# Neighbourhood attention in a hybrid encoder block: a fused bias sum and row maximum, one broadcast normalisation, attention steps in mid-projection, merge additions on VectorE

## The chip, the cores and the metric

The kernel runs on one core of a Trainium2 chip. The metric is the device time of one execution in microseconds (us). A core has five engines that run side by side, each through its own instruction list in order: TensorE (PE, matmuls, with PEld for its weight loads), VectorE (DVE), ScalarE (ACT), GpSimd (POOL) and SyncE (SP, which here issues most DMAs). They wait for one another on semaphores.

## The reference

One layer of an encoder block on 512 tokens of width 1024, in float32. Cut to what matters here:

```python
h = rms_norm(x, mix_norm_g)
proj = h @ w_in            # mLSTM q,k,v,o,gates | attention q,k,v | memory q | merge gates
y_ml = mlstm_branch(...)                         # branch 0 of the kernel
y_xa = memory_cross_attention(xa_q, mem_k, mem_v)   # branch 1
y_na = neighbourhood_attention(na_q, na_k, na_v, na_rpb)   # branch 2
merged = g_ml * (y_ml @ w_br_ml) + g_na * (y_na @ w_br_na) + g_xa * (y_xa @ w_br_xa)
x = x + merged @ w_out
x = x + conv_glu_ffn(rms_norm(x, ffn_norm_g), ...)
return rms_norm(x, final_norm_g)
```

In the neighbourhood attention the tokens form a grid of 8 rows by 64 columns, and there are 8 heads of 64 channels. A token sees all 8 rows and a window of 16 columns; a learned bias, indexed by the relative position, is added to the scores before the softmax:

```python
s = einsum('bhrcd,bhrkjd->bhrckj', q, k_band) * 64 ** -0.5 + bias
s = where(col_ok, s, -inf)
p = softmax(s over all keys of the token)
o = einsum('bhrckj,bhrkjd->bhrcd', p, v_band)
```

The gates `g_*` are sigmoids of 1024 projected channels each.

## The kernel before, in words

Activations lie transposed: 128 channels on the partitions, 512 tokens along the free axis. Float32 accuracy is got from the faster fp32r matmul by splitting both operands into a high and a low part (`wh`, `wl` for weights, `XH`, `XL` for the input); `mm3` (L181) then issues three matmuls, L182, L183 and L184. A projection (`proj`, L328) of one 128-channel block is 8 input tiles by 3 matmuls, 24 matmuls of 128x512, into a PSUM tile `mm`. The weights come as a list of blocks; `weights` (L170) keeps three raw loads (`wr`) and one split ahead. A split is an ACT copy (L164) and a DVE subtraction (L165) for each half block.

The branches are written as generators (`ml_all`, `xa_all`, `na_all`) that yield at the end of each of their steps. `step(n)` (L786) adds n to a quota and runs one generator step for each whole unit. So the generators' work is sprinkled between projections. The instruction lists that result are reordered a little by the scheduler that builds the program, so that some matmuls of a projection come to stand between parts of a step.

The merge loop (L857 to L892) runs over three branches `br`, and for each over four feature pairs `fp`. A pair consists of two gate projections, each followed on DVE by L872 and on ACT by a tanh (L873), and by `step(RATE[br])`; then come two branch projections of 12 matmuls each (L886) and again `step(RATE[br])`. `RATE` is 0.85, 1.6 and 0. While `br` is 0 (mLSTM merge) the steps are those of the cross-attention; while `br` is 1 (cross-attention merge) they are those of the neighbourhood attention; while `br` is 2 nothing is stepped. The merged sum lies in SBUF tiles `mg` (a `u` in the profile): branch 0 writes it, and branches 1 and 2 form gate times projection on DVE (L890) and add it to the sum on GpSimd (L891).

`na_all` (L602) has 18 steps over 16 score tiles; a tile t is one head and half of the queries' column blocks, 128 rows by two blocks of 256 keys. Step t

- issues the load of the bias tile t+1 (`nab`, two buffers, SP queue, L629);
- computes the scores of tile t: four matmuls of 128x256 (L642, L643) into a PSUM tile `at`; DVE adds the bias (L644), DVE takes the negated row maximum of each half (L646), ACT takes the exponential of each half with its row sum (L649), DVE takes the reciprocal (L650) and scales each half by it (L652);
- every fourth step, prepares the operands of the next two heads (`prep`, L609: ACT L618 to L620, DVE L621 and L622);
- multiplies the values of tile t-2 (L671), and for odd tiles stores the result of a head (ACT L679, DVE L680);
- transposes the probabilities of tile t-1 on TensorE (L658) and copies them to SBUF, on ACT for even tiles (L661) and on DVE for odd ones (L663).

TensorE executes its list in order. A transposition whose probabilities are not ready, or a value product whose copy is not ready, holds up all matmuls behind it.

Of the kernel before, what the change touches and what calls it, by code (L numbers as in the profile page):

```python
# [14 lines left out]
ALU = mybir.AluOpType  # L15
AX = mybir.AxisListType

P = 128
S = 512
D = 1024  # L20
KT = D // P
NT = S // P
M = 256
# [5 lines left out]
RATE = (0.85, 1.6, 0)  # L29
EPS = 1e-6  # L30
NEG = -1e30
# [64 lines left out]
def hybrid_block(ctx, tc, xT, memT, wflat, vecs, gbias, nabias, outa, outb):  # L96
    nc = tc.nc
    V, A, G, PE, SY = nc.vector, nc.scalar, nc.gpsimd, nc.tensor, nc.sync
# [82 lines left out]
    def mm3(ps, lh, ll, rh, rl, start, stop):  # L181
        PE.matmul(ps, lh, rh, start=start, stop=False)  # L182
        PE.matmul(ps, lh, rl, start=False, stop=False)  # L183
        PE.matmul(ps, ll, rh, start=False, stop=stop)  # L184
# [89 lines left out]
    XH = [hx[k // 4][:, (k % 4) * S:(k % 4 + 1) * S] for k in range(KT)]  # L274
    XL = [hx[2 + k // 4][:, (k % 4) * S:(k % 4 + 1) * S] for k in range(KT)]
# [49 lines left out]
        V.scalar_tensor_tensor(c, th, 1.0, c, op0=ALU.add, op1=ALU.mult)  # L325
        split_act(dst[0][:, sl], dst[1][:, sl], c)

    def proj(key, XHs, XLs, n=S):  # L328
        ws = weights(key)
        ps = mmps()  # L330
        for k in range(KT):
            mm3(ps[:, :n], ws[k][0], ws[k][1], XHs[k], XLs[k], k == 0, k == KT - 1)
        return ps

# [4 lines left out]
    for f in range(4):  # L339
        ps = proj(("mlk", f), XH, XL)  # L340
# [28 lines left out]
    for c in range(4):  # L369
        if c == 3:  # L370
            mem_part()
        n = 272 if c == 0 else 256
        pss = [(mmps if c % 2 else atps)() for _ in range(NT)]
        for h in range(2):
            ws = weights(("tm", c, h))
            for t in range(NT):
                tsl = slice(t * P, (t + 1) * P)
                for k in range(4):
                    kk = 4 * h + k
                    ps = pss[t][:, :n]  # L380
                    mm3(ps, XH[kk][:, tsl], XL[kk][:, tsl], ws[k][0], ws[k][1], kk == 0, kk == KT - 1)
        for t in range(NT):
            ps = pss[t]
# [218 lines left out]
    def na_all(nq, nk, yh, yl):  # L602

        QZ = [[tp.tile([P, S], F32R, tag="H", name=nm("QZ"), bufs=4) for _ in range(2)] for _ in range(2)]
        for pair in QZ:
            for e in range(2):
                G.memset(pair[e][64 - 64 * e:128 - 64 * e].bitcast(F32), 0.0)

        def prep(hp):  # L609
            qn = nq[:, hp * S:(hp + 1) * S]  # L610
            kn = nk[:, hp * S:(hp + 1) * S]
            QL = QZ[hp % 2]
            QS, KS = [], []
            for e in range(2):
                own, oth = slice(64 * e, 64 * e + 64), slice(64 - 64 * e, 128 - 64 * e)
                q2 = tp.tile([P, S], F32R, tag="R", name=nm("QS"), bufs=4)
                k2 = tp.tile([P, S], F32R, tag="R", name=nm("KS"), bufs=4)
                A.activation(q2[own], qn[own], AF.Copy)  # L618
                A.activation(k2[own], kn[own], AF.Copy)
                A.activation(q2[oth], qn[own], AF.Copy)  # L620
                V.tensor_tensor(k2[oth], kn[own], k2[own].bitcast(F32), op=ALU.subtract)  # L621
                V.tensor_tensor(QL[e][own], qn[own], q2[own].bitcast(F32), op=ALU.subtract)  # L622
                QS.append(q2)
                KS.append(k2.rearrange("p (r w) -> p r w", r=ROWS))
            return QS, KS, QL

        def bias_tile(i):
            bt = tp.tile([P, 2 * M], F32, tag="nab", name=nm("nab"))
            SY.dma_start(bt, nabias[i // 2, i % 2])  # L629
            return bt  # L630

        def scores(i, ops, bt):
            QS, KS, QL = ops
            e, bp = (i // 2) % 2, i % 2
            ps = atps()
            sm = scr()
            mx = tiny(2)
            for j in range(2):
                b = 2 * bp + j
                bs = slice(b * P, (b + 1) * P)  # L640
                ks = KS[e][:, :, CW[b]:CW[b] + 32]
                PE.matmul(ps[:, j * M:(j + 1) * M], QS[e][:, bs], ks, start=True, stop=False)  # L642
                PE.matmul(ps[:, j * M:(j + 1) * M], QL[e][:, bs], ks, start=False, stop=True)  # L643
            V.tensor_tensor(sm, ps, bt, op=ALU.add)  # L644
            smv = sm.rearrange("p (a b) -> p a b", a=2)
            V.tensor_reduce(mx, smv, axis=AX.X, op=ALU.max, negate=True)  # L646
            su = tiny(2)
            for j in range(2):
                A.activation(smv[:, j, :], smv[:, j, :], AF.Exp, bias=mx[:, j:j + 1], accum_out=su[:, j:j + 1])  # L649
            V.reciprocal(su, su)  # L650
            for j in range(2):
                V.tensor_scalar(smv[:, j, :], smv[:, j, :], su[:, j:j + 1], None, op0=ALU.mult)  # L652
            return sm

        def transposes(i, sm):
            pt = atps()
            for j in range(4):
                PE.transpose(pt[:, j * P:(j + 1) * P], sm[:, j * P:(j + 1) * P], ident)  # L658
            ptS = scr()
            if i % 2 == 0:  # L660
                A.activation(ptS, pt, AF.Copy)  # L661
            else:
                V.tensor_copy(ptS, pt)  # L663
            return ptS

        def values(i, ptS, py):

            h, bp = i // 2, i % 2
            for j in range(4):
                b, hf = 2 * bp + j // 2, j % 2  # L670
                PE.matmul(py[:, b, :], vwin(b, hf, h // 2), ptS[:, j * P:(j + 1) * P], start=hf == 0, stop=hf == 1)  # L671

        def store(h, py):

            hs, es = slice(h // 2 * S, (h // 2 + 1) * S), slice(64 * (h % 2), 64 * (h % 2) + 64)
            pyv = py[es].rearrange("p b (r c) -> p b r c", r=ROWS)
            yhv = yh[es, hs].rearrange("p (r b c) -> p b r c", r=ROWS, b=4)
            ylv = yl[es, hs].rearrange("p (r b c) -> p b r c", r=ROWS, b=4)
            A.activation(yhv, pyv, AF.Copy)  # L679
            V.tensor_tensor(ylv, pyv, yhv.bitcast(F32), op=ALU.subtract)  # L680

        n = 16
        ops = prep(0)
        bt = bias_tile(0)
        sms, pts, py = {}, {}, None
        yield
        for t in range(n + 2):
            if t < n:
                nb = bias_tile(t + 1) if t + 1 < n else None
                sms[t] = scores(t, ops, bt)  # L690
                bt = nb
                if t % 4 == 3 and t + 1 < n:
                    ops = prep((t + 1) // 4)
            i = t - 2
            if 0 <= i:
                if i % 2 == 0:
                    py = atps().rearrange("p (b q) -> p b q", b=4)
                values(i, pts.pop(i), py)
                if i % 2 == 1:
                    store(i // 2, py)  # L700
            i = t - 1
            if 0 <= i < n:
                pts[i] = transposes(i, sms.pop(i))
            yield
# [81 lines left out]
    def step(n=1):  # L786
        quota[0] += n
        while quota[0] >= 1 and gens:
            try:
                next(gens[0])  # L790
                quota[0] -= 1
            except StopIteration:
                gens.pop(0)
        if not gens:
            quota[0] = 0.0
# [6 lines left out]
    for f in range(4):  # L802
        ps = proj(("xaq", f), XH, XL)
# [6 lines left out]
    for f in range(4):  # L810
        ps = proj(("o", f), XH, XL)
# [45 lines left out]
    for br in range(3):  # L857
        gi = (0, 2, 1)[br]
        if br == 0:
            ys[1] = [unit(F32R), unit(F32R)]  # L860
            gens.append(xa_all(xq, mk, mv, *ys[1]))
        if br == 1:
            load_vwin()
            ys[2] = [unit(F32R), unit(F32R)]
            gens.append(na_all(nq, nk, *ys[2]))
        for fp in range(4):
            tg = []
            for i in range(2):
                f = 2 * fp + i
                ps = proj(("g", br, f), XH, XL)  # L870
                t = scr()
                V.tensor_tensor(t, ps, rb, op=ALU.mult)  # L872
                A.activation(t, t, AF.Tanh, scale=0.5, bias=mgbh[:, gi * 8 + f:gi * 8 + f + 1])  # L873
                tg.append(t)
                step(RATE[br])
            drain(tags[br])
            if br == 0 and not mg:
                mg.extend([unit(), unit()])
            yh, yl = ys[br]
            ws = weights(("br", br, fp))  # L880
            for i in range(2):
                f = 2 * fp + i
                ps = mmps()
                for k in range(4):
                    ks, fs = slice(k * S, (k + 1) * S), slice(i * P, (i + 1) * P)
                    mm3(ps, ws[k][0][:, fs], ws[k][1][:, fs], yh[:, ks], yl[:, ks], k == 0, k == 3)  # L886
                if br == 0:
                    V.scalar_tensor_tensor(mgv(f), tg[i], 1.0, ps, op0=ALU.add, op1=ALU.mult)
                else:
                    V.scalar_tensor_tensor(tg[i], tg[i], 1.0, ps, op0=ALU.add, op1=ALU.mult)  # L890
                    G.tensor_tensor(mgv(f), mgv(f), tg[i], op=ALU.add)  # L891
            step(RATE[br])  # L892
    mhu = [unit(F32R) for _ in range(4)]
    GH = [mhu[k // 4][:, (k % 4) * S:(k % 4 + 1) * S] for k in range(KT)]
# [247 lines left out]
```

## Time and profile before

| | |
|---|---|
| three runs | 917.39, 918.46, 918.47 us; median 918.46 |
| profiled execution | 917.16 us, its span 915.4 us |
| TensorE busy | 899.7 us (98% of the span), granted clock 0.998 |
| VectorE busy | 577.7 us (63%) |
| ScalarE busy | 437.7 us (48%) |
| GpSimd busy | 135.0 us (15%) |
| DMA moved | 96.39 MB, mean 105 GB/s |

How to read it: the span is that of the instructions of one execution; 1.76 us of the execution's time lie outside it. Matmuls are pipelined, and each record is about 0.39 us long while the next one starts 0.23 us after it; so the space between the starts of two matmuls tells more of a stall than the busy share does. In the timeline, the columns are start, duration, engine, line, operation and tiles, with the idle time before the instruction and what ended it in brackets. In the groups by line, they are the busy time, the mean duration in nanoseconds, and the idle time before with its releasers.

### The profile page before, as it was taken

To read this page: it belongs to the slowest core of one execution; us is meant where nothing else is said; L and a number is where in the kernel's file an instruction comes from. 1 tells how busy PE (TensorE), PEld (TensorE's weight loads), DVE (VectorE), ACT (ScalarE), POOL (GpSimd) and SP (SyncE) were. 2 spreads that over 40 slices of the span, in tenths; PEclk is the share of its full clock that TensorE was granted. 3 is DMA by queue.
4 is the path that set the end of the run, shared out by engine and by line. 5 is a ranking of instruction groups with operands and counts; after the bars stand their busy time and mean duration, and the time that the engine had idled before them with its cause. 6 is when DMAs were issued, how large, how long until landed. Compare 5 with 4: busy or idle time off the path is not lost.

```text
span 915.4 us, 12086 instructions
## 1 busy us (share of the span) xinstructions
PE 899.7 (98%) x4431; PEld 750.8 (82%) x4431; DVE 577.7 (63%) x993; ACT 437.7 (48%) x879; POOL 135.0 (15%) x158
## 2 busy tenths in 40 slices
PE   7999999999999999999999999999999999999996
PEld 5899878888888888788888888888888888888886
DVE  7893665746566668895454548777733477777333
ACT  7464546655545557563334435444422344444442
POOL 6000321102040300111111221111100011111112
PEclk9999999999999999999999999999999999999999
DMA  7223522422231423232223332222222322222322
GB/s 256 96 93 106 189 98 101 155 92 90 81 127 73 134 81 125 83 127 70 93 92 116 137 116 92 92 93 93 85 95 95 115 93 92 93 93 86 95 72 92
DMA packets 32939, 96.39 MB, mean 105 GB/s; under 512 B 4056, under 2 KB 7528, under 8 KB 32880
## 3 DMA queue, kind: packets, MB, share of 16 engines
q1 hardware_dynamic: 31440, 92.45, 29.2%
q0 software_dynamic: 1440, 3.17, 1.2%
q8 instruction: 35, 0.57, 0.3%
q14 instruction: 24, 0.20, 0.1%
HBM read 92.44 MB, written 3.16 MB: 104 GB/s over the span
## 4 chain that ended last, share of the span: by engine, by line
PE 95%; DVE 2%; issue 1%; DMA 0%; ACT 0%; POOL 0%; SPq 0%; POOLq 0%; DVEq 0%; ACTq 0%
PE mm L182 28%; PE mm L183 28%; PE mm L184 28%; PE at L535 2%; PE at L182 2%; PE at L183 2%; PE at L184 2%; PE at L671 1%; PE at L658 1%; DMA wr<-wflat 0%; POOL u L979 0%; PE at L748 0%; PE at L642 0%; PE at L643 0%; DVE s L890 0%
## 5 line engine op out<-in xcount | busy, mean ns | idle before, releaser
L182 PE MATMUL mm<-u,wh 128*128 128x512 f32 (+1 forms) x1115 | 435.8, 391 | 5.4 <-ACT wh L164 5.3
L184 PE MATMUL mm<-u,wl 128*128 128x512 f32 (+1 forms) x1115 | 433.2, 389 | 0.0
L183 PE MATMUL mm<-u,wh 128*128 128x512 f32 (+1 forms) x1115 | 433.0, 388 | 0.0
L164 ACT ACTIVATE wh<-wr 128x512 fp32r<-128x512 f32 (+3 forms) x305 | 189.5, 623 | 298.4 <-PE mm L183 262.6
L165 DVE TENSOR_TENSOR wl<-wr,wh 128x512 fp32r<-128x512 f32 (+3 forms) x305 | 234.4, 770 | 145.2 <-ACT wh L164 141.0
L182 PEld LDWEIGHTS mm<-u,wh 128*128 128x128 f32 x1115 | 209.9, 188 | 50.8 <-ACT wh L164 6.2
L184 PEld LDWEIGHTS mm<-u,wl 128*128 128x128 f32 x1115 | 209.8, 188 | 45.9
L183 PEld LDWEIGHTS mm<-u,wh 128*128 128x128 f32 x1115 | 209.9, 188 | 44.8 <-DVE u L189 0.5
L1012 POOL TENSOR_TENSOR s<-s,rb 128x512 f32<-128x512 f32 x22 | 29.1, 1324 | 266.4 <-DVE s L1011 258.3
L891 POOL TENSOR_TENSOR u<-u,s 128x512 f32<-128x512 f32 x16 | 22.4, 1399 | 166.1 <-DVE s L890 108.9
L188 ACT ACTIVATE u<-s 128x512 fp32r<-128x512 f32 x34 | 21.4, 629 | 52.3 <-DVE s L1015 50.6
L872 DVE TENSOR_TENSOR s<-mm,rb_x 128x512 f32<-128x512 f32 x24 | 16.6, 692 | 28.8 <-PE mm L184 28.8
L189 DVE SCALAR_TENSOR_TENSOR u<-s,u 128x512 fp32r<-128x512 f32 x34 | 23.5, 692 | 14.7 <-ACT u L188 14.4
L523 ACT ACTIVATE E<-R,bi 128x128 f32<-128x128 f32 x80 | 27.8, 394 | 4.7 <-POOL R L504 4.2
L317 ACT ACTIVATE s<-pad,vec 128x512 f32<-128x512 f32 x30 | 24.4, 813 | 8.3 <-DVE pad L315 8.3
L318 DVE SCALAR_TENSOR_TENSOR s<-pad,vec,s 128x512 f32<-128x512 f32 x30 | 22.5, 750 | 6.1 <-ACT s L317 6.1
L182 PE MATMUL mm<-wh,u 128*128 128x256 f32 (+1 forms) x80 | 24.5, 306 | 0.0
L1026 DVE TENSOR_TENSOR u<-mm,u 128x512 f32<-128x512 f32 (+1 forms) x17 | 11.2, 659 | 20.8 <-PE mm L184 20.8
L183 PE MATMUL mm<-wl,u 128*128 128x256 f32 (+1 forms) x80 | 24.3, 304 | 0.0
L184 PE MATMUL mm<-wh,u 128*128 128x256 f32 (+1 forms) x80 | 24.3, 304 | 0.0
L1011 DVE SCALAR_TENSOR_TENSOR s<-s,s 128x512 f32<-128x512 f32 x22 | 15.2, 692 | 13.4 <-ACT s L1010 13.3
L319 DVE SCALAR_TENSOR_TENSOR s<-pad,vec,s 128x512 f32<-128x512 f32 x30 | 22.5, 749 | 0.7
(230 smaller groups left out, 911.1 us busy)
## 6 DMA issues: line engine op xcount, KB each, us to landing
wr<-wflat SPq DMA_DIRECT2D x141, 512.0 KB, 3.2
s<-xT SPq DMA_DIRECT2D x16, 256.0 KB, 4.0
nab<-nabias SPq DMA_DIRECT2D x16, 256.0 KB, 2.7
wr<-wflat SPq DMA_DIRECT2D x17, 192.0 KB, 2.3
R<-rd SPq DMA_DIRECT2D x8, 256.0 KB, 3.5
u<-nav_d POOLq DMA_DIRECT2D x32, 64.0 KB, 3.0
wr<-wflat SPq DMA_DIRECT2D x2, 544.0 KB, 3.2
s<-memT SPq DMA_DIRECT2D x4, 256.0 KB, 3.7
```

Of the source, the lines that this page charges most:

```text
L164: A.activation(h[:, u:v], src, AF.Copy)
L165: V.tensor_tensor(l[:, u:v], src, h[:, u:v].bitcast(F32), op=ALU.subtract)
L182: PE.matmul(ps, lh, rh, start=start, stop=False)
L183: PE.matmul(ps, lh, rl, start=False, stop=False)
L184: PE.matmul(ps, ll, rh, start=False, stop=stop)
L189: V.scalar_tensor_tensor(l, src, scale, h.bitcast(F32), op0=ALU.mult, op1=ALU.subtract)
L317: A.activation(t1, pad[:, 0:512], AF.Identity, scale=vcol(w, i), bias=vcol(b, i))
L318: V.scalar_tensor_tensor(t1, pad[:, 1:513], vcol(w, n + i), t1, op0=ALU.mult, op1=ALU.add)
L319: V.scalar_tensor_tensor(t1, pad[:, 2:514], vcol(w, 2 * n + i), t1, op0=ALU.mult, op1=ALU.add)
L523: A.activation(E[:, i, :], src, AF.Exp, bias=bi[:, d, abs(J - s), s, h:h + 1])
L891: G.tensor_tensor(mgv(f), mgv(f), tg[i], op=ALU.add)
L1012: G.tensor_tensor(c, c, rb2, op=ALU.mult)
```

## The change

Four edits:

1. The bias sum and the row maximum become one instruction for each half: `tensor_tensor_reduce` writes scores plus bias and accumulates the maximum. It is emitted as a VectorE instruction of its own kind, 128x256, followed by an instruction that reads the accumulator into the 128x1 result. The sign of the maximum is then turned by a 128x2 instruction (before, the reduction negated it).
2. The two scalings by the reciprocal become one `tensor_tensor` of 128x512 whose second operand is the pair of reciprocals, broadcast along the keys.
3. `proj` takes a function that it calls in the middle of its 24 matmuls. The gate projections pass half a step's quota there, and the other half follows at the old place.
4. The addition to the merge sum goes from GpSimd to VectorE.

```diff
-    def proj(key, XHs, XLs, n=S):
+    def proj(key, XHs, XLs, n=S, mid=None):
         ws = weights(key)
         ps = mmps()
         for k in range(KT):
+            if mid and k == KT // 2:
+                mid()
             mm3(ps[:, :n], ws[k][0], ws[k][1], XHs[k], XLs[k], k == 0, k == KT - 1)
         return ps
...
-            V.tensor_tensor(sm, ps, bt, op=ALU.add)
             smv = sm.rearrange("p (a b) -> p a b", a=2)
-            V.tensor_reduce(mx, smv, axis=AX.X, op=ALU.max, negate=True)
+            for j in range(2):
+                js = slice(j * M, (j + 1) * M)
+                V.tensor_tensor_reduce(smv[:, j, :], ps[:, js], bt[:, js], 1.0, 2.0 * NEG, ALU.add, ALU.max,
+                                       accum_out=mx[:, j:j + 1])
+            V.tensor_scalar(mx, mx, -1.0, None, op0=ALU.mult)
             su = tiny(2)
             for j in range(2):
                 A.activation(smv[:, j, :], smv[:, j, :], AF.Exp, bias=mx[:, j:j + 1], accum_out=su[:, j:j + 1])
             V.reciprocal(su, su)
-            for j in range(2):
-                V.tensor_scalar(smv[:, j, :], smv[:, j, :], su[:, j:j + 1], None, op0=ALU.mult)
+            V.tensor_tensor(smv, smv, su.unsqueeze(2).to_broadcast([P, 2, M]), op=ALU.mult)
             return sm
...
-                ps = proj(("g", br, f), XH, XL)
+                ps = proj(("g", br, f), XH, XL, mid=lambda: step(RATE[br] / 2))
...
-                step(RATE[br])
+                step(RATE[br] / 2)
...
-                    G.tensor_tensor(mgv(f), mgv(f), tg[i], op=ALU.add)
+                    V.tensor_tensor(mgv(f), mgv(f), tg[i], op=ALU.add)
```

In the changed file the lines below the first edit stand two further on and those below the second four: the fused instruction is L649, the sign L651, the exponential L654, the reciprocal L655, the normalisation L656, the DVE copy L667, gate times projection L894 and the addition L895.

## The prediction

> **What bounds the kernel now.** I read the page first, then the busy time by stretches, then TensorE's timeline where it loses time, then DVE's and POOL's at those places, and last the groups by shape for prices.
>
> ```profile
> span 915.4 us, 12086 instructions
> ...
> PE 899.7 (98%) x4431; PEld 750.8 (82%) x4431; DVE 577.7 (63%) x993; ACT 437.7 (48%) x879; POOL 135.0 (15%) x158
> ...
> PE 95%; DVE 2%; issue 1%; DMA 0%; ACT 0%; POOL 0%; SPq 0%; POOLq 0%; DVEq 0%; ACTq 0%
> ```
>
> TensorE carries 95% of the chain that ended last. The change adds and removes no matmul; it can only win time in which TensorE stands still, or make more of it. The stretches tell where that is (258 to 336.8 us: cross-attention steps; 336.8 to 425: neighbourhood attention steps; then branch 2 of the merge). The columns are the length, the busy time of PE, PEld, DVE, ACT and POOL with their instructions, the granted clock and the DMAs:
>
> ```profile
> 258.00:336.80 78.80, 78.80 (x382) 65.55 (x382) 51.19 (x111) 41.89 (x97) 14.71 (x30) 1.00 0.32 107
> 336.80:425.00 88.20, 86.10 (x494) 72.85 (x494) 76.75 (x143) 53.61 (x125) 10.37 (x8) 1.00 0.30 102
> 425.00:500.00 75.00, 75.00 (x330) 61.10 (x329) 35.22 (x53) 28.43 (x46) 12.01 (x9) 1.00 0.29 100
> ```
>
> TensorE is never idle on either side of the attention stretch; so half steps in the cross-attention, and additions on DVE in branch 2 (DVE busy 35 of 75 us), have nothing to win. In the attention stretch it idles 2.1 us and DVE is busy for 87%. The columns of the next rows are start, duration, engine, line, tiles, and the idle time with its releaser:
>
> ```profile
> 346.61 0.39 PE L184 MATMUL mm<-u,wl 128*128 128x512 f32 x1
> 346.84 0.40 PE L182 MATMUL mm<-u,wh 128*128 128x512 f32 x1
> ...
> 348.01 0.40 PE L184 MATMUL mm<-u,wl 128*128 128x512 f32 x1
> 349.03 0.63 PE L658 MATMUL at<-ident,s 128*128 128x128 f32 x4 [0.62 <-DVE s L652]
> ...
> 364.47 0.40 PE L183 MATMUL mm<-u,wh 128*128 128x512 f32 x1
> 364.89 0.63 PE L658 MATMUL at<-ident,s 128*128 128x128 f32 x4
> ...
> 369.56 1.05 PE L671 MATMUL at<-s,u 128*128 128x128 f32 x8
> 370.45 0.60 PE L658 MATMUL at<-ident,s 128*128 128x128 f32 x4
> 370.81 0.37 PE L642 MATMUL at<-KS,QS 128*128 128x256 f32 x1
> ...
> 371.37 0.39 PE L182 MATMUL mm<-u,wh 128*128 128x512 f32 x1
> ...
> 372.30 0.40 PE L183 MATMUL mm<-u,wh 128*128 128x512 f32 x1
> 373.90 1.16 PE L671 MATMUL at<-s,u 128*128 128x128 f32 x8 [1.21 <-DVE s L663]
> ...
> 389.87 0.40 PE L183 MATMUL mm<-u,wh 128*128 128x512 f32 x1
> 390.45 1.16 PE L671 MATMUL at<-s,u 128*128 128x128 f32 x8 [0.18 <-ACT s L661]
> ```
>
> Matmuls of 128x512 follow each other at 0.23 us (346.61 to 346.84). What the next start lies beyond that is the loss: 0.79 at 349.03, 0.19 at 364.89, 1.37 at 373.90, 0.35 at 390.45; 2.7, and with slow restarts (1.16 where such a group takes 1.05) and smaller ones some 3 us: the ceiling of the gain. The rows from 369.56 on also show a step's other work: values 0.89, transposition 0.36, scores 0.56 (370.81 to 371.37). DVE is the releaser of the two large ones, and this is why it was late:
>
> ```profile
> 341.10 1.29 POOL L891 TENSOR_TENSOR u<-u,s 128x512 f32<-128x512 f32 x1 [34.80 <-DVE y L650]
> ...
> 341.13 1.68 DVE L652 TENSOR_SCALAR s<-s,y 128x256 f32<-128x256 f32 x2
> ...
> 343.33 0.68 DVE L890 SCALAR_TENSOR_TENSOR s<-s,mm 128x512 f32<-128x512 f32 x1
> 343.93 0.68 DVE L644 TENSOR_TENSOR s<-at,nab 128x512 f32<-128x512 f32 x1
> 344.53 1.41 DVE L165 TENSOR_TENSOR wl<-wr,wh 128x512 fp32r<-128x512 f32 x1
> ...
> 347.16 0.69 DVE L621 TENSOR_TENSOR KS<-u,KS 64x512 fp32r<-64x512 f32 x1
> 347.87 0.17 DVE L650 RECIPROCAL y<-y 128x2 f32<-128x2 f32 x1
> 347.96 0.67 DVE L646 TENSOR_REDUCE y<-s 128x2 f32<-128x512 f32 x1
> 348.54 0.61 DVE L652 TENSOR_SCALAR s<-s,y 128x256 f32<-128x256 f32 x2
> ...
> 370.06 0.67 DVE L890 SCALAR_TENSOR_TENSOR s<-s,mm 128x512 f32<-128x512 f32 x1
> ```
>
> Two scalings take 0.61 us alone and 1.68 beside a POOL addition. Two DVE instructions of 0.68 follow each other at 0.60, a small one is followed after 0.09 (347.87 to 347.96), one that must wait for its forerunner starts at its end (0.71 after L621's start).
>
> **The change, part by part.** Prices (groups: busy us, mean ns, idle before): the first three rows from the attention stretch, the next three from the cross-attention stretch, a scan of the mLSTM preparation, and three of ACT's timeline:
>
> ```profile
> L165 DVE TENSOR_TENSOR wl<-wr,wh 128x512 fp32r<-128x512 f32 x21 | 16.1, 769 | 1.9 <-ACT wh L164 1.9
> L652 DVE TENSOR_SCALAR s<-s,y 128x256 f32<-128x256 f32 x32 | 13.0, 446 | 0.3
> L646 DVE TENSOR_REDUCE y<-s 128x2 f32<-128x512 f32 x16 | 10.8, 675 | 0.1
> ...
> L165 DVE TENSOR_TENSOR wl<-wr,wh 128x512 fp32r<-128x512 f32 x23 | 15.8, 687 | 11.7 <-ACT wh L164 11.7
> ...
> L189 DVE SCALAR_TENSOR_TENSOR s<-at,s 128x256 fp32r<-128x256 f32 x16 | 6.2, 419 | 0.8 <-ACT s L188 0.2
> ...
> L741 DVE TENSOR_SCALAR s<-s,y 128x256 f32<-128x256 f32 x16 | 4.9, 351 | 0.2
> ...
> L454 DVE TENSOR_TENSOR_SCAN s<-s,at 4x512 f32<-4x512 f32 x1 | 1.2, 1222 | 0.0
> ...
> 325.44 0.72 ACT L188 ACTIVATE s<-at 128x256 fp32r<-128x256 f32 x2 [0.48 <-DVE s L189]
> ...
> 346.56 0.51 ACT L649 ACTIVATE s<-s,y 128x256 f32<-128x256 f32 x1 [0.81 <-DVE y L646]
> ...
> 347.07 0.49 ACT L649 ACTIVATE s<-s,y 128x256 f32<-128x256 f32 x1
> ```
>
> *Fused bias sum and maximum.* No trace row shows it. Out go L644 and L646, 0.60 each from start to start: 1.20 for a tile. In come two halves, each with an accumulator read, and a sign flip (0.09). A half as a plain 128x256 instruction is 0.42 long and followed after 0.42 - 0.08 = 0.34. ACT's exponentials with an accumulator read follow at 0.51 (346.56 to 347.07), plain ones at 0.72 - 0.39 = 0.33: 0.18 for accumulating. I take 0.34 + 0.18 = 0.52, the pair 1.04, since that is the row of the same kind of work. Low end: accumulating is free, pair 0.68. High end: the fused instruction runs at the scan's rate, (1.22 - 0.16) / 512 columns, 0.53 + 0.16 a half, with ACT's 0.18 for the read: pair 1.74.
>
> *Broadcast normalisation.* 0.53 to the next start (0.61 less 0.08) becomes a two-input 128x512 one, as L890: 0.60 in the queue, 0.69 for the reader. In the queue a tile costs 1.04 + 0.09 + 0.60 = 1.73 against 1.20 + 0.53 = 1.73: nothing, for 16 tiles.
>
> *Additions to DVE.* Eight fall in this stretch, 8 x 0.60 = 4.8 us more for DVE. The POOL additions go, and with them what they cost DVE: (769 - 687) x 21 + (446 - 351) x 32 = 1.7 + 3.0 = 4.7 us. So this is nothing in sum too, but the delay leaves the places where it hurt. [...] Eight more additions lie in branch 2, where DVE is 53% idle and TensorE waits for nothing; POOL has nothing queued behind them there.
>
> *Half steps.* The order of the changed instruction lists can be followed. Before, two steps often stand back to back after a projection: the scores of tile t and the transposition of tile t are then parted by little TensorE work. Now 12 or 24 matmuls stand between any two steps, but for the first three tiles, whose order stays. From the scores of a tile to its transposition TensorE has in the usual case values 0.9, transposition 0.4, 12 matmuls 2.8, scores 0.5, values 0.9: 5.5 us. The chain it must cover is the pair and the sign, 1.13, an exponential pair 1.0 and its last read 0.18, reciprocal 0.17, normalisation 0.69, and three strangers in DVE's queue at 0.6: 5.0. Slack 0.5. Each step also issues the bias load of the next tile on SP, now half a projection earlier against the weight loads; it waits there for the fused instruction that frees a buffer, and weight loads behind it are three blocks ahead of use (over 8 us), so I cost it at nothing; if that cover went, a wait would show on L182. Nothing of a step is queued on POOL but the zeroing ahead of the first.
>
> Now the stalls one by one.
> - 349.03 (0.79): TensorE now has 12 matmuls ahead of this transposition, not 9, and is there at 348.24 + 0.69 = 348.93. DVE from 343.33: L890 0.60, half 0.52, addition 0.60, half 0.52, weight split 0.60, sign 0.09, operand 0.70, pair 1.04, reciprocal 0.09, operand 0.60, normalisation 0.69: 349.38. Three more matmuls done, 0.35 later: gain 0.34.
> - 364.89 and 390.45 (0.19, and 0.35 with 0.11 for the slow restart): back-to-back steps, now 12 matmuls apart. Gain 0.65.
> - 373.90 (1.37 and 0.11): the odd copy L663 stood behind L890 at 370.06, which POOL had pushed back. Now L890 starts when its matmuls end (369.2), then half, addition, half, copy: 369.2 + 0.60 + 0.52 + 0.60 + 0.52 + 0.69 = 372.13. TensorE, with 3 matmuls ahead instead of 5, is there at 371.37 + 0.69 = 372.06. Gain 1.41.
>
> Sum 2.4 us. The profiled execution of 917.16 (915.4 span, 1.76 outside it) would become 914.8; it is 1.30 below the median, so against the median I forecast 918.46 - 2.4 = 916.1. A run less than 0.2% (1.84 us) away can hardly be told from no change.
>
> **The rivals.**
>
> *The stalls only move.* The additions stand on DVE between the two halves of a fused pair, at the very places of the large stalls; with the slack of 0.5 us used up by one more stranger (0.6) the 0.34 and half of the 1.41 are lost, and a new 0.2 appears at three steps: 2.4 - 0.3 - 0.7 - 0.6 = 0.8, 917.7. For it: DVE is busy for 87% and no work leaves it. Against it: of the losses listed none lies behind 391 us, in the last 34 us of the stretch.
>
> *Every instruction pays its whole length.* The softmax of a tile goes from five DVE instructions to seven. If the new kind doesn't overlap with its successor, a half is 0.42 + 0.16 and the pair 1.16; the pair stands in the three chains four times (two in the first), so 4 x 0.12 and another 0.2 for the sign: gain 1.7, 916.8. For it: dependent instructions do follow at full length. Against it: 0.60 and 0.09 above. [...]
>
> *Slower: the fused instruction runs at the scan's rate.* Pair 1.74. DVE then gets 16 x 0.70 = 11.2 us more, and 11.45 us is all that it idles in the stretch (88.2 - 76.75). DVE becomes the bound: with a third of its idle time staying, since the chains begin with waits for TensorE and ACT, the stretch grows by 11.2 - 7.6 = 3.6: 922.1. The gain is gone from a pair of 1.64 on (0.6 in excess, four times). For it: the scan also feeds each result back. Against it: the reduction, which accumulates too, runs at 675 for 512 columns.
>
> **How the numbers follow.** Forecast 0.50 (its own range 915.3 to 917.0, from pair 0.9 to 1.2), stalls move 0.20, whole length 0.12, scan rate 0.18. Faster by over 0.2%: the forecast less a tail of 0.03, 0.47. Slower: scan rate and a tail, 0.20. The rest, 0.33, within. The range goes from 914.8 (all 3 us won, and the run-to-run 0.6) to 920.4, which takes the lower half of the scan case in and leaves 0.1 above and some 0.05 below.
>
> **What would show it.** Right: the fused group near 0.42 us with reads of 0.16 or less, its halves 0.5 apart; no L652 or L165 of 1.4 us in the stretch; TensorE's idle time there under 1 us; the wait of 1.21 on the copy gone. Wrong: fused instructions above 0.6 us; waits of L662 or L675 on DVE L656 or L667 at many steps; DVE above 95% there. The forecast fails if the halves are dear, or if the idle time goes to other steps; if the stalls are gone and time stays, my reading of TensorE's starts was wrong.

## The result

| | kernel before | changed kernel |
|---|---|---|
| median of 15 runs | 917.95 us (917.14 to 918.48) | 915.80 us (915.16 to 916.75) |
| ratio | | 0.9979, 95% interval 0.9972 to 0.9985 |
| profiled execution, its span | 917.16, 915.4 us | 916.23, 914.3 us |
| VectorE busy in 336.8 to 425 us | 76.75 us | 71.32 us |
| TensorE idle there | 2.10 us | 0.18 us |

The change makes the kernel 2.15 us faster. Of the changed kernel's page, these lines answer to those shown of before: the span, the engines' busy time, and the shares of the chain that ended last.

```profile
span 914.3 us, 12085 instructions
...
PE 899.5 (98%) x4431; PEld 751.9 (82%) x4431; DVE 580.0 (63%) x1041; ACT 437.7 (48%) x879; POOL 112.6 (12%) x142
...
PE 96%; DVE 1%; ACT 1%; DMA 0%; POOL 0%; issue 0%; SPq 0%; POOLq 0%; DVEq 0%; ACTq 0%
```

The two spans differ by only 1.1 us, because each profiled execution has its own start: the first matmul began at 5.30 us in the one before and at 6.13 in the changed one, 0.83 later. To compare traces free of that, I take two landmarks in the middle of TensorE's work, the 301st matmul of 128x512 and the last of them (there are 3307 in either kernel). TensorE's timeline of the kernel before has them here:

```profile
126.69 0.40 PE L183 MATMUL mm<-u,wh 128*128 128x512 f32 x1
...
895.72 0.39 PE L184 MATMUL mm<-u,wl 128*128 128x512 f32 x1
```

and that of the changed kernel here:

```profile
127.52 0.40 PE L183 MATMUL mm<-u,wh 128*128 128x512 f32 x1
...
894.26 0.39 PE L184 MATMUL mm<-u,wl 128*128 128x512 f32 x1
```

769.03 us became 766.74: TensorE gained 2.29 us between them. Below, this distance is called the way between the landmarks. Each kernel was profiled in one execution, so the distance has no interval; but from the 301st to the 735th of these matmuls, ahead of what the edits change, all the profiles of this document agree within 0.02 us (131.55 to 131.57). From the 1035th to the 1280th (337.35 to 425.21 us before, 338.09 to 423.42 in the changed kernel), the attention stretch, 87.86 us became 85.33, 2.53 less. The stretch ahead of it gained 0.09, and from the 1561st to the 1761st (491 to 537 us) 46.22 us became 46.49, with no wait of TensorE in the profile. By stretches (length; busy PE, PEld, DVE, ACT, POOL; granted clock; DMAs) the changed kernel reads

```profile
258.00:336.80 78.80, 78.80 (x382) 65.38 (x381) 51.73 (x112) 42.17 (x97) 15.49 (x32) 1.00 0.35 107
336.80:425.00 88.20, 88.02 (x505) 75.70 (x504) 71.32 (x183) 53.60 (x125) 0.00 (x0) 1.00 0.33 107
425.00:500.00 75.00, 75.00 (x330) 61.03 (x330) 40.30 (x62) 28.86 (x46) 0.00 (x0) 1.00 0.31 100
```

GpSimd does nothing any more from 336.8 to 500 us; TensorE was never idle in the stretches shown on either side of the attention stretch, as before. VectorE took the additions over and is nevertheless busy for 5.4 us less. Its groups in the attention stretch (busy us, mean ns, idle time before and its releasers):

```profile
L165 DVE TENSOR_TENSOR wl<-wr,wh 128x512 fp32r<-128x512 f32 x21 | 14.4, 686 | 3.4 <-ACT wh L164 1.7 <-PE at L645 1.5
L649 DVE CUSTOM_DVE_ANT_0 s<-at,nab 128x256 f32<-128x256 f32 x32 | 12.5, 418 | 0.0
L656 DVE TENSOR_TENSOR s<-s,y 128x512 f32<-128x512 f32 x16 | 11.0, 689 | 0.4
L895 DVE TENSOR_TENSOR u<-u,s 128x512 f32<-128x512 f32 x8 | 5.5, 689 | 0.1
...
L649 DVE DVE_READ_ACCUMULATOR2_ANT y<- 128x1 f32 x32 | 2.7, 83 | 0.0
```

The weight splits (L165) are back at 686 ns from 769, the value of the undisturbed stretch. A fused half is 418 ns, its accumulator read 83. What these cost in the queue is in VectorE's timeline:

```profile
343.85 0.69 DVE L894 SCALAR_TENSOR_TENSOR s<-s,mm 128x512 f32<-128x512 f32 x1 [0.16 <-PE mm L184]
344.45 0.42 DVE L649 CUSTOM_DVE_ANT_0 s<-at,nab 128x256 f32<-128x256 f32 x1
344.80 0.08 DVE L649 DVE_READ_ACCUMULATOR2_ANT y<- 128x1 f32 x1
344.80 0.69 DVE L895 TENSOR_TENSOR u<-u,s 128x512 f32<-128x512 f32 x1
...
347.24 0.42 DVE L649 CUSTOM_DVE_ANT_0 s<-at,nab 128x256 f32<-128x256 f32 x1
347.59 0.08 DVE L649 DVE_READ_ACCUMULATOR2_ANT y<- 128x1 f32 x1
347.59 0.42 DVE L649 CUSTOM_DVE_ANT_0 s<-at,nab 128x256 f32<-128x256 f32 x1
347.93 0.08 DVE L649 DVE_READ_ACCUMULATOR2_ANT y<- 128x1 f32 x1
347.93 0.16 DVE L655 RECIPROCAL y<-y 128x2 f32<-128x2 f32 x1
348.01 0.67 DVE L624 TENSOR_TENSOR QZ<-u,QS 64x512 fp32r<-64x512 f32 x1
348.60 0.68 DVE L656 TENSOR_TENSOR s<-s,y 128x512 f32<-128x512 f32 x1
```

The read starts at the same time as the instruction behind it (344.80, 347.93): accumulating takes no place in the queue, and a pair costs 347.93 - 347.24 = 0.69 us. TensorE's timeline at the places where it stood still before:

```profile
349.45 0.39 PE L184 MATMUL mm<-u,wl 128*128 128x512 f32 x1
349.68 0.60 PE L662 MATMUL at<-ident,s 128*128 128x128 f32 x4
...
371.64 0.40 PE L184 MATMUL mm<-u,wl 128*128 128x512 f32 x1
371.88 1.12 PE L675 MATMUL at<-s,u 128*128 128x128 f32 x8
...
375.14 0.40 PE L183 MATMUL mm<-u,wh 128*128 128x512 f32 x1
375.72 0.63 PE L662 MATMUL at<-ident,s 128*128 128x128 f32 x4 [0.18 <-DVE s L656]
```

The transposition and the value product that had lost 0.79 and 1.37 us now follow at the usual 0.23. One stall of 0.35 (0.58 - 0.23) is there at 375.72, on a normalisation. Summed over 330 to 430 us, the distances between starts, less a usual 0.23 us after a matmul of 128x512, 0.12 after 128x256 and 0.11 after 128x128, make 3.96 us in the kernel before and 1.36 in the changed one. Each sum hangs on the usual distance taken (with 0.232 it is 0.6 lower); the difference of 2.6 does not. The 0.35 is the only stall over 0.15 that the changed kernel has left there.

### The profile page after: what moved, and what is told of

It is laid out like the page before. It is cut to its first block, busy times and chain, and to the rows that moved or that the text cites. A ratio compares the mean times of both kernels' runs of the same rounds, so it can differ in the third digit from the quotient of the medians.

```text
span 914.3 us, 12085 instructions
## 1 busy us (share of the span) xinstructions
PE 899.5 (98%) x4431; PEld 751.9 (82%) x4431; DVE 580.0 (63%) x1041; ACT 437.7 (48%) x879; POOL 112.6 (12%) x142
## 4 chain that ended last, share of the span: by engine, by line
PE 96%; DVE 1%; ACT 1%; DMA 0%; POOL 0%; issue 0%; SPq 0%; POOLq 0%; DVEq 0%; ACTq 0%
PE mm L182 28%; PE mm L183 28%; PE mm L184 28%; PE at L537 2%; PE at L182 2%; PE at L183 2%; PE at L184 2%; PE at L675 1%; PE at L662 1%; DMA wr<-wflat 0%; POOL u L983 0%; PE at L752 0%; PE at L644 0%; PE at L645 0%; PE at L561 0%
## 5 line engine op out<-in xcount | busy, mean ns | idle before, releaser
L165 DVE TENSOR_TENSOR wl<-wr,wh 128x512 fp32r<-128x512 f32 (+3 forms) x305 | 235.6, 774 | 142.9 <-ACT wh L164 137.1
L921 POOL TENSOR_TENSOR acc<-acc,s 128x512 f32<-128x512 f32 x7 | 9.1, 1295 | 223.8 <-ACT s L920 223.8
```

Source lines behind the costliest of these rows:

```text
L165: V.tensor_tensor(l[:, u:v], src, h[:, u:v].bitcast(F32), op=ALU.subtract)
```

## The experiments

Three theories were put up ahead of the first four runs: the gain needs both VectorE free of GpSimd and the half steps (1), it comes from the half steps' spacing (2), or from GpSimd's delay of VectorE alone (3; the expectations call it the lock: two scalings took 1.68 us beside an addition on GpSimd and 0.61 without one). The table has every run; ratios are against the kernel before, measured beside them on the same chip (its median 917.53 us beside the first four, 917.59 beside the four marked b, 917.77 beside the three marked c). The fourth column is the way between the landmarks in the profiled execution, 769.03 before, and the last one what changed of it in the attention stretch, 87.86 before.

| kernel | median us | ratio, 95% interval | landmarks us | in the stretch us |
|---|---|---|---|---|
| half steps alone | 917.91 | 1.0006 (0.9997 to 1.0014) | 768.84 (-0.19) | -0.02 |
| additions on VectorE alone | 915.70 | 0.9978 (0.9969 to 0.9987) | 766.91 (-2.12) | -2.48 |
| the two softmax edits alone | 917.71 | 1.0003 (0.9994 to 1.0012) | 768.26 (-0.77) | -0.80 |
| all but the half steps | 916.67 | 0.9988 (0.9979 to 0.9996) | 767.06 (-1.97) | -2.32 |
| additions back beside (GpSimd into a junk tile), b | 923.15 | 1.0061 (1.0048 to 1.0073) | 773.83 (+4.80) | +4.08 |
| all but the move of the additions, b | 916.85 | 0.9993 (0.9984 to 1.0002) | 768.06 (-0.97) | -0.77 |
| half steps and additions, c | 915.85 | 0.9978 (0.9969 to 0.9988) | 766.73 (-2.30) | -2.53 |
| no additions at all, c | 916.93 | 0.9992 (0.9983 to 1.0001) | 767.61 (-1.42) | -1.74 |
| additions, last scaling on VectorE, b | 916.24 | 0.9985 (0.9976 to 0.9994) | 766.90 (-2.13) | -2.46 |
| changed kernel, last scaling on VectorE, b | 916.53 | 0.9988 (0.9979 to 0.9997) | 766.71 (-2.32) | -2.56 |
| the same, scaling and its transfers first, c | 915.46 | 0.9975 (0.9965 to 0.9984) | 766.72 (-2.31) | -2.53 |

The medians hold more than TensorE's work. An execution's part outside the span is steady within a kernel and differs between kernels: about 1.77 us before, 1.90 in the changed kernel, 2.11 with the half steps alone, 2.09 without them, 2.30 in the last row. Why it differs is not shown. So the order of variants a few tenths apart is read from the traces.

### Each edit alone

Half steps alone:

```diff
-                ps = proj(("g", br, f), XH, XL)
+                ps = proj(("g", br, f), XH, XL, mid=lambda: step(RATE[br] / 2))
...
-                step(RATE[br])
+                step(RATE[br] / 2)
```

> Only the half steps in mid-projection; old softmax, additions on GpSimd. Theory 1 (spacing and the lock both count): the two stalls between back-to-back steps (0.19 and 0.46 us with the restart) go, the two behind GpSimd's additions stay in part: gain 1.0 to 1.5 us, TensorE idle 0.8 to 1.2 us in the attention stretch. Theory 2 (spacing alone): gain 2.0 to 2.5 us, TensorE idle under 0.5 us. Theory 3 (the lock alone): gain 0.6 us at most.

No gain. The waits of TensorE in the attention stretch (total us, times, longest) show both large stalls still there, and a second one at the transposition:

```profile
PE at L673 <- DVE s L665: 1.2, 1, 1.2
PE at L660 <- DVE s L654: 1.0, 2, 0.6
```

The small stalls at 364 and 390 us are gone, but a new one of 0.53 has come at 402. What the half steps take away at two places they give back at a third.

Additions on VectorE alone:

```diff
-                    G.tensor_tensor(mgv(f), mgv(f), tg[i], op=ALU.add)
+                    V.tensor_tensor(mgv(f), mgv(f), tg[i], op=ALU.add)
```

> Only the additions to the merge buffer on VectorE. Theory 1: gain 0.3 to 0.8 us; no VectorE instruction of 1.4 us is left in the attention stretch, and the stall of 1.37 us at the odd copy falls by about half, since two additions of 0.6 us stand where 1.07 and 0.7 us of lock were. Theory 2: gain 0.2 us at most. Theory 3: gain 1.5 us or more, both large stalls gone.

By the medians this is the whole gain, 1.83 us, and theory 3's range holds it. With the old softmax and whole steps, only one of TensorE's three waits in that stretch is left:

```profile
PE at L671 <- ACT s L661: 0.2, 1, 0.2
```

The two softmax edits alone:

```diff
-            V.tensor_tensor(sm, ps, bt, op=ALU.add)
-            V.tensor_reduce(mx, smv, axis=AX.X, op=ALU.max, negate=True)
+            for j in range(2):
+                V.tensor_tensor_reduce(smv[:, j, :], ps[:, js], bt[:, js], 1.0, 2.0 * NEG, ALU.add, ALU.max,
+                                       accum_out=mx[:, j:j + 1])
+            V.tensor_scalar(mx, mx, -1.0, None, op0=ALU.mult)
...
-                V.tensor_scalar(smv[:, j, :], smv[:, j, :], su[:, j:j + 1], None, op0=ALU.mult)
+            V.tensor_tensor(smv, smv, su.unsqueeze(2).to_broadcast([P, 2, M]), op=ALU.mult)
```

> Only the fused bias sum and maximum and the broadcast normalisation. Priced by the changed kernel's own rows (a fused half every 0.34 us, so 0.68 for a pair where 1.20 was; normalisation 0.60 where 0.53 was) VectorE has 0.36 us less per tile. Theory 1: gain 0.3 to 0.8 us. Theories 2 and 3: gain 0.2 us at most.

The stalls become shorter and stay:

```profile
PE at L673 <- DVE s L665: 0.8, 1, 0.8
PE at L660 <- DVE s L654: 0.5, 1, 0.5
PE at L673 <- ACT s L663: 0.2, 1, 0.2
```

The trace has TensorE 0.77 us better between the landmarks; the times do not show it, and their interval allows a gain of 0.55 us at most. So the trace falls into theory 1's range, and the time into that of theories 2 and 3.

All but the half steps:

```diff
-                ps = proj(("g", br, f), XH, XL, mid=lambda: step(RATE[br] / 2))
+                ps = proj(("g", br, f), XH, XL)
...
-                step(RATE[br] / 2)
+                step(RATE[br])
```

> The whole change but for the half steps. Theory 1: gain 0.8 to 1.3 us; the stalls between back-to-back steps stay (0.2 and 0.5 us), those behind the additions are smaller. Theory 2: gain 0.3 us at most. Theory 3: gain 1.8 us or more.

The large stalls are gone here too. By the landmarks the gain is 1.97 us, as theory 3 has it; by the medians it is only 0.86, as theory 1 has it. Of the 1.1 us between the two, 0.3 is the longer part outside the span, and the rest is not explained. Half steps are worth 0.32 us in the trace on top of this kernel (767.06 to 766.74), 0.18 on top of the additions alone (766.91 to 766.73, below), 0.20 on top of the softmax edits (768.26 to 768.06, below), 0.19 alone; in the attention stretch it is 0.21, 0.05, -0.03 and 0.02. Theory 2 falls, since the half steps alone leave both large stalls. Theory 3 stands by the additions alone; of theory 1 there remain two or three tenths.

### The pairs, and the delay put back

Half steps and additions, with the old softmax:

```diff
-                ps = proj(("g", br, f), XH, XL)
+                ps = proj(("g", br, f), XH, XL, mid=lambda: step(RATE[br] / 2))
...
-                    G.tensor_tensor(mgv(f), mgv(f), tg[i], op=ALU.add)
+                    V.tensor_tensor(mgv(f), mgv(f), tg[i], op=ALU.add)
```

> The kernel before with the half steps and the additions on VectorE; the softmax is the old one. Theory 1 (the additions leaving GpSimd are the whole gain, the half steps nothing): as the additions alone, 915.4 to 916.2, ratio 0.998; TensorE loses 1.0 to 1.7 us start to start in the attention stretch, and the stall at the transposition that the half steps alone had at 402 is back or stays. Rival (half steps are worth their 0.65 us once the long instructions are gone): 914.9 to 915.3, TensorE loses under 1 us there.

It is equal to the changed kernel in time and in the trace (766.73 against 766.74). So the softmax edits, worth 0.77 alone, are worth nothing once the additions are off GpSimd: both had been buying the same two stalls. Theory 1 of this run holds by its time, its ratio and TensorE's loss in the stretch (1.36 us); the stall that it expected at 402 is not there, one of 0.38 stands at 374.50 instead.

All but the move of the additions:

```diff
-                    V.tensor_tensor(mgv(f), mgv(f), tg[i], op=ALU.add)
+                    G.tensor_tensor(mgv(f), mgv(f), tg[i], op=ALU.add)
```

> The changed kernel with its additions left on GpSimd: fused sum and maximum, broadcast normalisation and half steps together. Theory 1 (GpSimd's hold on VectorE is the whole of it): the long instructions of VectorE (1.3 to 1.7 us) stay, TensorE still loses 2.8 to 4 us in the attention stretch, time 917.2 to 918.2, ratio 0.9995 to 1.0005. Rival (the three other edits work only together, since the half steps space the softmaxes and the fused pair shortens each): TensorE loses under 2 us there, time 916.0 to 916.6, ratio 0.9985.

The time and its ratio came out a little below theory 1's ranges (916.85 for 917.2 to 918.2, 0.9993 for 0.9995 to 1.0005), though the ratio's interval reaches into them; the loss in the stretch, 3.15 us, is inside. The rival's loss under 2 us did not come, nor its time. Six instructions of VectorE over 1 us are still in the stretch; with the additions on VectorE there is none.

The delay put back, nothing moved:

```diff
+    junk = cp.tile([P, S], F32, name="junk")
+    G.memset(junk, 0.0)
...
                     V.tensor_tensor(mgv(f), mgv(f), tg[i], op=ALU.add)
+                    G.tensor_tensor(junk, junk, tg[i], op=ALU.add)
```

> The changed kernel with every addition still on VectorE, and behind each of the eight additions one more on GpSimd, of the same gate tile into a tile that nothing reads. [...] Theory 1 (the change gained because GpSimd no longer holds VectorE up in these places): in the attention stretch instructions of VectorE of 1.3 to 1.7 us come back, TensorE loses 2.5 to 4 us there start to start instead of the changed kernel's 1.4, and the time goes back to 917 to 918.5, ratio to the kernel before 0.999 to 1.0005. Theory 2 (the gain comes from where the addition stands in VectorE's order, or from GpSimd's reply that the next use of the buffer waited for): no difference from the changed kernel, 915.6 to 916.0, ratio 0.998.

The direction is theory 1's and the size beyond it: 7.35 us slower than the changed kernel, 5.6 slower than before. All sixteen additions have one beside them, eight of them in branch 2. Nothing reads the junk tile. In the attention stretch TensorE, VectorE and ScalarE have the same instructions in the same order as in the changed kernel, and the profile shows none that waits for GpSimd, so only GpSimd's presence acts. GpSimd's timeline has the addition here,

```profile
372.90 1.29 POOL L898 TENSOR_TENSOR junk<-junk,s 128x512 f32<-128x512 f32 x1 [1.29 <-DVE s L896]
```

and VectorE's, beside it:

```profile
373.02 1.71 DVE L897 TENSOR_TENSOR u<-u,s 128x512 f32<-128x512 f32 x1
374.65 0.41 DVE L649 CUSTOM_DVE_ANT_0 s<-at,nab 128x256 f32<-128x256 f32 x1
375.00 0.08 DVE L649 DVE_READ_ACCUMULATOR2_ANT y<- 128x1 f32 x1
375.00 0.68 DVE L667 COPY s<-at 128x512 f32<-128x512 f32 x1
```

VectorE's addition takes 1.71 us beside GpSimd's instead of 0.69, and the copy behind it, for which TensorE waits, comes a microsecond late. Every second of VectorE's additions is hit like this (1.70 to 1.78 us, the others 0.69; L897 has a mean of 1201 ns in the stretch, where the changed kernel has 689), and beside the others GpSimd hits the instruction behind them, a normalisation of 1.78 or a weight split of 1.77 and 1.64. Why it is worse than before the change is not shown in full: the stretch has six instructions of VectorE over 1 us, before it had seven; but VectorE now has its own additions to do as well, and three of the delays reach TensorE, which loses 1.6 us at 351.42, 2.1 at 375.73 and 1.7 at 407.84. And one stall cost more than itself:

```profile
373.41 0.40 PE L184 MATMUL mm<-u,wl 128*128 128x512 f32 x1
375.73 1.76 PE L675 MATMUL at<-s,u 128*128 128x128 f32 x8 [1.93 <-DVE s L667]
377.14 0.77 PE L182 MATMUL mm<-u,wh 128*128 128x512 f32 x1
377.71 0.63 PE L183 MATMUL mm<-u,wh 128*128 128x512 f32 x1
378.14 0.63 PE L184 MATMUL mm<-u,wl 128*128 128x512 f32 x1
```

The matmuls after it start 0.43 us apart instead of 0.23; more on this below. The way between the landmarks grew by 7.09 us against the changed kernel, 6.6 of it in the attention stretch.

No additions at all (branches two and three are computed and not added to the merge sum, so the output lacks them):

```diff
-                    G.tensor_tensor(mgv(f), mgv(f), tg[i], op=ALU.add)
```

> The kernel before without the sixteen merge additions, on any engine: branches two and three are computed and not added, so the output lacks them. Theory 1 (on VectorE the additions cost nothing, their 0.60 us each lies beside TensorE's work): the same as the additions on VectorE alone, 915.3 to 916.0, ratio 0.998, TensorE's loss in the attention stretch 1.0 to 1.5 us. Rival (they delay VectorE where TensorE waits for it): up to 1 us less, 914.6 to 915.2.

Neither held: it is slower than with the additions on VectorE, 916.93 against 915.70 (each beside its own runs of the kernel before; the intervals of the two ratios overlap, 0.9983 to 1.0001 and 0.9969 to 0.9987), and by 0.70 us in the trace. Without the additions the merged sum is complete after branch 0, and the scheduler brings the eight splits of it (8 instructions of VectorE, 5.4 us, and 8 of ScalarE, 4.9 us) forward into the attention stretch; VectorE is busy there for 76.22 us against 75.70 with the additions. TensorE has stalls of 0.19, 0.51, 0.35 and 0.18 us at 364, 374, 388 and 406. So the run took no work from VectorE in this stretch and cannot price the additions. That VectorE's amount of work is not what sets the time is shown by two other runs: the softmax edits alone bring it to 70.44 us and win 0.80 us in the stretch, the additions alone leave it at 75.70 and win 2.48.

### A version that should beat both

In the changed kernel's last microseconds GpSimd scales four of eight output tiles and VectorE three beside it, at 0.7 instead of 0.34 us each; the addition of the last projection (905.26 us) waits behind these three. First all eight on VectorE, in the kernel with the additions alone and in the changed one:

```diff
-            (V, G)[i % 2].tensor_tensor(x2[i][:, :a], x2[i][:, :a], rbs, op=ALU.mult)
+            V.tensor_tensor(x2[i][:, :a], x2[i][:, :a], rbs, op=ALU.mult)
```

> The kernel before with the additions on VectorE and with the last scaling of the eight output tiles all on VectorE instead of in turn on VectorE and GpSimd. The profile of the changed kernel has GpSimd's four scalings near the end at about 0.9 us each, with VectorE's three beside them at 0.7 instead of 0.34. [...] If the end is set by the transfers of the output or by the last matmuls: no difference from the kernel with the additions alone, 915.5 to 916.0, ratio 0.998.

> The changed kernel with the last scaling of the eight output tiles all on VectorE. If GpSimd's hold on VectorE costs there too: 914.3 to 915.1, about 1 us below the changed kernel, ratio to the kernel before 0.9965. If the end is set by the transfers of the output or by the last matmuls: 915.5 to 916.1, ratio 0.998.

VectorE's scalings are short again (three in 1.10 us, in the changed kernel 2.17) and TensorE's last matmul starts sooner (in the changed kernel 907.40 us, 906.47 with this edit, and the first matmul 6.13 and 5.99), but the time did not fall: 916.24 and 916.53 us lie above every range expected. The issues of the output's transfers show why. In the changed kernel the last four are

```profile
908.78 1.81 SPq L981 DMA_DIRECT2D outb<-s  x4
```

and in the changed kernel with the scaling on VectorE

```profile
907.97 1.82 SPq L981 DMA_DIRECT2D outb<-s  x4
909.88 0.51 SPq L985 DMA_DIRECT2D outa<-u  x1
```

One scaling stood last on VectorE, behind its two instructions for the other half, and its transfer went out last. So the scaling and its transfers were written ahead of the other half's:

```diff
+        for i in range(KT):
+            V.tensor_tensor(x2[i][:, :a], x2[i][:, :a], rbs, op=ALU.mult)
+        for i in range(0, KT, 4):
+            SY.dma_start(outa[i * P:(i + 4) * P, :].rearrange("(f p) s -> p f s", p=P), x2v[i // 4][:, :, :a])
         for t in range(nt):
             for g in range(2):
                 o = scr()
...
-        for i in range(KT):
-            (V, G)[i % 2].tensor_tensor(x2[i][:, :a], x2[i][:, :a], rbs, op=ALU.mult)
```

> The changed kernel with the last scaling of the eight output tiles all on VectorE, and written, with its two output transfers, ahead of the last half's own scaling and transfers instead of behind them. In the run with the scaling on VectorE alone, one scaling stood behind VectorE's last two instructions and its transfer was the last to be issued, at 909.9 us, which took back the 0.9 us by which the last tile's addition was earlier. If that order was what took it back: the last issue comes 0.7 to 1 us earlier than in the changed kernel, and the time is 914.7 to 915.2, ratio 0.997. If the end is set otherwise (by the landing of the transfers, whichever is last): 915.5 to 916.2, ratio 0.998.

```profile
905.10 2.36 SPq L977 DMA_DIRECT2D outa<-u  x2
907.96 2.43 SPq L985 DMA_DIRECT2D outb<-s  x4
```

The last four issues begin 0.82 us sooner than in the changed kernel, but take 2.43 us for 1.81 and end at 910.39 against 910.59; the view of the transfers has the four at 3.0 us to landing instead of 2.4. They begin 0.50 us after the end of the two issues ahead of them, for 1.58 in the changed kernel, and most of what VectorE gave is taken back. Whether the smaller gap is the cause, no run tests. By the medians of all runs the span did fall by 0.7 us (913.9 to 913.2), and the part outside it grew by 0.4. The time, 915.46 us, lies between the two ranges and decides for neither. With a ratio of 0.9975, this is the fastest kernel of the study; its interval overlaps that of the changed kernel, so that it beats it is not shown.

## Why the prediction was right, and where its steps were not

The forecast was 916.1 us, 2.4 below the kernel before; measured were 2.15 by the medians and 2.29 by the landmarks. The mechanism was right. Some terms were not: the stall at 349.03 gave more than its term, the half steps far less, and 0.27 us were lost behind the stretch. These errors cancelled, so that the sum came so near is in part luck.

- *TensorE loses only in the attention stretch, about 3 us.* Right: 3.96 by starts, of which 1.36 is left. One thing moved outside the stretch: the 200 matmuls from 491 to 537 us take 46.49 us for 46.22. Every kernel with the additions on VectorE has this (46.49, with the delay put back 46.99), and none without them (46.21 to 46.22). TensorE waits for nothing there, and the cause is open.
- *The delay by GpSimd leaves the places that hurt.* Right, and it is nearly all of the gain (-2.12 of -2.29). I had written that the sum on VectorE would not change (4.8 against 4.7 us); with the additions alone its busy time in the stretch is 75.70 against 76.75. What counted was where the time had been. The delay shows in both directions: L165 has a mean of 686 ns with GpSimd away, for 769 before, and an addition takes 1.71 us for 0.69 with GpSimd back beside it.
- *Fused pair 1.04.* Mis-sized: it is 0.69, my low end. I had added the 0.18 that ACT pays for its accumulator read. The nearer row stood in the same fence: VectorE's own reduction, which accumulates too, at 675 ns for 512 columns, as long as an instruction that does not (the bias sum L644, 679 ns). With it fell the rival of the scan's rate and that of the whole length. In the queue fusing does save time: pair, sign and normalisation take 0.69 + 0.09 + 0.60 = 1.38 us where 1.73 were. In the result these 0.35 us for a tile do not show once the additions are on VectorE.
- *Normalisation 0.60 in the queue, 0.69 for the reader.* Right (689 ns).
- *349.03, gain 0.34.* Too small: the stall is gone. From the start of gate times projection to the end of the normalisation I had 6.05 us; it took 349.28 - 343.85 = 5.43, the difference being the halves at 0.35 instead of 0.52. Nor was my reason for the 12 matmuls (half steps) right: with half steps alone there are still 9 and the stall is 0.79; with the additions alone there are 9 and none; and the kernel without half steps, which has the other three edits, has 12.
- *364.89 and 390.45, gain 0.65 from the half steps.* This is the step that failed. Both stalls go in the changed kernel, but a wait of 0.35 comes at 375.72, and in the run with half steps alone one of 0.53 at 402. Between the landmarks the half steps are worth 0.18 to 0.32 us by four comparisons, in the attention stretch -0.03 to 0.21, and nothing that the times can show. I had put the stalls taken away into the sum and not asked what would be late next. At 375.72 it is the slack of 0.5 us that was wrong. The second half of that tile's fused pair and its normalisation stand in VectorE's timeline at

```profile
370.76 0.42 DVE L649 CUSTOM_DVE_ANT_0 s<-at,nab 128x256 f32<-128x256 f32 x1
...
374.88 0.69 DVE L656 TENSOR_TENSOR s<-s,y 128x512 f32<-128x512 f32 x1
```

  with six other instructions between them (a copy, a weight split, the next tile's pair, two operands), where my chain had three strangers in all. The kernel without half steps waits there too (0.29 us at 375.83), so this one is not of their making.
- *373.90, gain 1.41.* Right: the copy L667 starts at 371.10 and is 0.69 long, its value product starts at 371.88 without a wait. But it needs only the additions, not the shorter pair: with the additions alone there is no stall on L663.
- *The stalls only move.* True of the half steps, not of the large stalls. The additions do stand between the halves of a pair, as this rival said (344.80), and did no harm; VectorE is down to 81% (71.32 of 88.20 us).

## What to carry to other kernels

Look for instructions of one engine that are twice as long as their kind (here a weight split of 1.41 us for 0.69), and see what another engine does at that moment: moving that work over can win although the receiving engine's sum of work stays nearly the same (VectorE 75.70 us in the stretch with the additions alone, 76.75 before). Before adding up the gains of several edits, ask which stalls each of them removes; here -2.12, -0.77 and -0.19 us alone made -2.29 together, since they bought the same two stalls. Where the time's scatter is as large as the effect, the distance of two landmark instructions in the traces leaves out the start and what lies outside the span; it comes from one execution, so it should be read together with the waits that explain it, and it did not always agree with the medians here. And a run that only leaves work out has to be read for what the scheduler puts in its place.

## What was not expected of the hardware

- The fused instruction's accumulator is free in the queue: the read (83 ns) starts together with the next instruction, 0.34 us after the fused half began (347.59 to 347.93).
- TensorE's clock fell after a short stall. In the run with the delay put back, by stretches of 3.41 us counted from the place where it fell:

```profile
348.80:352.22 3.42, 1.97 (x13) 1.43 (x12) 3.27 (x11) 2.19 (x8) 0.00 (x0) 1.00 0.90 299
372.70:376.11 3.41, 1.48 (x10) 1.00 (x9) 3.41 (x9) 1.47 (x3) 1.29 (x1) 1.00 0.00 0
376.11:379.52 3.41, 3.41 (x13) 2.93 (x13) 3.29 (x11) 3.07 (x10) 0.00 (x0) 0.50 0.78 251
403.42:406.83 3.41, 2.86 (x19) 2.39 (x17) 3.30 (x9) 1.80 (x6) 0.00 (x0) 1.00 0.27 77
406.83:410.24 3.41, 2.40 (x13) 2.08 (x14) 2.79 (x10) 1.08 (x4) 0.00 (x0) 1.00 0.57 187
```

  The granted clock (third column from the end) was 0.50 for 3.41 us, right behind a stretch of that length in which TensorE was busy for 1.48 us and waited 1.93; by starts it cost about 1 us more. The waits of 1.5 us at 351 and of 1.6 at 406 in the same run left it at 1.00. The second of these falls into two such stretches, and TensorE was busy in them for 2.86 and 2.40 us; in that of the first it was busy for 1.97. One such event was seen in mid-kernel, so what brings it on stays open.
